# Sums of weight blocks kept as a rounded and a low half, in a three-stage hybrid layer on one core

## The chip, the cores and the metric

The kernel runs on one core of one Trainium2 chip. The metric is the device time of one execution in microseconds (us), as the median of several runs. PE is TensorE's matmul, PEld its weight load, DVE is VectorE, ACT ScalarE, POOL GpSimd, SP SyncE, which here only issues DMAs. "SPq" and "POOLq" are the DMA queues that SP and POOL feed.

## The reference, cut to what matters

One layer is applied to 2048 prompt tokens and to 64 tokens of a running sample. Nearly all the arithmetic is in matrix products with weights of 1024 rows:

```python
h = rms_norm(x, g_pre)
vA, bA, cA, zA, q, f, iv, zB, gA, gB = split_cols(h @ w_in)      # ten blocks of 1024 columns
yA = (silu(zA) * bA * causal_conv3(cA * vA)) @ w_a_out
S, o = hgrn2_scan(S0, silu(q) * scale, 1 - fg, iv, log(fg))      # chunks of 64 tokens, fg from f
yB = (norm(o) * g_onorm * silu(zB)) @ w_b_out
out = (sigmoid(gA) * yA + sigmoid(gB) * yB) @ w_o
x = x + rms_norm(out, g_post)
y = x + (p @ w_ple_proj) * sigmoid(rms_norm(x, g_ple) @ w_ple_gate)
```

All values are fp32.

## The kernel before, in words

**Products in three parts.** TensorE is fed in fp32r, a rounded fp32. So each fp32 operand is split into a rounded half `hi` and the remainder `lo` (`split`, lines 183 and 184: ACT rounds, DVE subtracts), and each product is made of three matmuls, hi with x_hi, hi with x_lo and lo with x_hi (lines 357 to 359, 490 to 492, 523 to 525). The weights are the stationary side, 128 x 128 at a time; a block of weights is a tile of 128 x 512, 256 KB: four 128 x 128 pieces. One such block with 352 tokens is twelve matmuls.

**Seven products for eight.** The 2112 tokens are cut into three blocks of 704, and each block into two halves of 352. Two weight columns (i1, i2), two halves of the depth and two halves of the tokens make a 2 x 2 by 2 x 2 product, which is done with seven block products in place of eight. Their weight sides are in `PRODUCTS` (lines 67 to 75), in the order A11, S3, S1, S2, A12, A22, S4. A11, A12 and A22 are blocks of the weights themselves. S1 to S4 are sums:

```
S1 = A21 + A22    S2 = S1 - A11    S3 = A11 - A21    S4 = A12 - S2
```

`sgroup` (line 343) does one such group. In blocks 1 and 2, `in_turn` (line 464) does W_A and W_B (in block 2 also W_O) product by product: all four groups' A11, then all their A12, then S2, S3, A22, S1 and S4 (`IN_TURN`, line 79), so four blocks of one kind stand in a row. The rest of W_O and the gate weights W_G go through plain `gemm`s.

**Keeping the sums.** Sums are made once. In block 0 `combined(first=True)` (line 286) loads four raw blocks, makes the four sums on DVE, and `keep_sum` (line 268) stores each sum to DRAM as plain fp32, splits it, and stores its low half (`split_w`, line 220). For W_A, W_B (in block 0) and W_O (in block 1) `prepare_sums` (line 303) does this beside other work, on POOL's queue; its `keep` (line 317) stores the sum, makes the low half in place and stores it. Later blocks load them: `kept_w` (line 274) loads the plain sum into a `raw` tile (line 194), ACT rounds it into a `hi` tile (line 214), and the low half is loaded into a `lo` or `s` tile (line 215). Blocks of the weights proper take the same way, from `w_blk`.

**Buffers.** All weight tiles are 128 x 512 of one pool `wp`: 5 for `raw`, 4 for `hi`, 4 for `lo`, 3 for `s` (`sum_tile`). Low halves in later blocks alternate between `lo` and `s` (`low_tile`, line 199), which gives seven buffers for seven products. A buffer is given out again once every reader of its last content is done. A scheduler lays out the order of each engine's instructions from dependences and priorities; every queue runs strictly in the order that results, so a DMA issue on SP that waits for a buffer holds up those behind it.

**Order of the work.** Block 0: `p @ w_ple_proj` for two blocks, heads with gates beside them (path B, to about 470 us of the span), path A (to about 690), the products with W_A, W_B and W_O by plain `gemm`s with `prepare_sums` beside them. Its last `gemm_by_k` (line 554) holds two weight columns, four `hi` tiles, to its end. Then gates of the next block (the first of them, `by_k`, line 361, goes through A11, S3, S1, S2 piece by piece), the end of the block with W_G, heads, path A, W_A and W_B in turn, W_O by plain `gemm`s; block 2 ends with W_A, W_B, W_O in turn, the last norm and W_G.

Of the kernel before, what the change touches and what calls it, by code (L numbers as in the profile page):

```python
# [10 lines left out]
F32 = mybir.dt.float32  # L11
F32R = mybir.dt.float32r
I32 = mybir.dt.int32
AF = mybir.ActivationFunctionType
ALU = mybir.AluOpType
# [3 lines left out]
P = 128  # L19
# [63 lines left out]
def hybrid_step(  # L83
# [17 lines left out]
    V, A, G, T, SP = nc.vector, nc.scalar, nc.gpsimd, nc.tensor, nc.sync  # L101
# [4 lines left out]
    wp = ctx.enter_context(tc.tile_pool(name="wp", bufs=4))  # L106
    ring = ctx.enter_context(tc.tile_pool(name="ring", bufs=RING))
    small = ctx.enter_context(tc.tile_pool(name="small", bufs=4))
    dram = ctx.enter_context(tc.tile_pool(name="dram", bufs=1, space=DRAM))
# [5 lines left out]
    def nm(s):  # L115
        uid[0] += 1
        return f"{s}_{uid[0]}"

    def rt(n=BN, dt=F32):
        t = ring.tile([P, BN + 4], dt, tag="r", name=nm("r"))  # L120
        return t if n is None else t[:, :n]
# [61 lines left out]
    def split(src, hi, lo):  # L183
        return A.copy(hi, src).ins, V.tensor_tensor(lo, src, hi.bitcast(F32), ALU.subtract).ins  # L184
# [7 lines left out]
    def load_raw(src):  # L192
        raw = wp.tile([P, 4, P], F32, tag="raw", name=nm("raw"), bufs=5)
        SP.dma_start(raw, src)
        return raw

    lows, turn = {}, [0]

    def low_tile():

        turn[0] += 1
        if turn[0] % 7 in (1, 3, 5):
            return sum_tile(F32R)
        return wp.tile([P, 4, P], F32R, tag="lo", name=nm("lo"))

    def sum_tile(dt=F32):
        return wp.tile([P, 4, P], dt, tag="s", name=nm("s"), bufs=3)

    def split_w(raw, key=None):

        hi = wp.tile([P, 4, P], F32R, tag="hi", name=nm("hi"))
        if key in lows:
            lo = low_tile()
            A.copy(hi, raw)  # L214
            SP.dma_start(lo.bitcast(F32), lows[key])
            return hi, lo
        lo = wp.tile([P, 4, P], F32R, tag="lo", name=nm("lo"))
        split(raw, hi, lo)
        if key is not None:
            lows[key] = dram.tile([P, 4, P], F32, tag=f"lo{key}", name=nm("low"), bufs=1)  # L220
            SP.dma_start(lows[key], lo.bitcast(F32))
        return hi, lo
# [42 lines left out]

    sums = {}

    def keep_sum(name, i1, s):

        sums.setdefault(i1, {})[name] = dram.tile([P, 4, P], F32, tag=f"{name}_{i1}", name=nm(name), bufs=1)  # L270
        SP.dma_start(sums[i1][name], s)
        return split_w(s, (i1, name))

    def kept_w(i1, i2, name, anew=False):

        keys = dict(A11=(i1, 0), A12=(i1, 1), A22=(i2, 1))
        if name in keys:
            return split_w(load_raw(w_blk[keys[name]]), None if anew else keys[name])
        return split_w(load_raw(sums[i1][name]), (i1, name))

    def combined(i1, i2, first):

        with tc.high_priority():
            if not first:
                return {n: kept_w(i1, i2, n) for _, n, _, _, _ in PRODUCTS}
            a11, a21, a22, a12 = (load_raw(w_blk[i, h]) for i, h in ((i1, 0), (i2, 0), (i2, 1), (i1, 1)))
            out = dict(A11=split_w(a11, (i1, 0)))

            def total(name, x, y, op):
                s = sum_tile()  # L290
                V.tensor_tensor(s, x, y, op)
                out[name] = keep_sum(name, i1, s)
                return s

            total("S3", a11, a21, ALU.subtract)
            s1 = total("S1", a21, a22, ALU.add)
            s2 = total("S2", s1, a11, ALU.subtract)
            out["A12"] = split_w(a12, (i1, 1))
            out["A22"] = split_w(a22, (i2, 1))
            total("S4", a12, s2, ALU.subtract)  # L300
            return out

    def prepare_sums(firsts, ahead):


        groups = [(idx + g, idx + KH + g) for idx in firsts for g in range(KH)]

        def tile_of(dt=F32):
            return rt(4 * P, dt).rearrange("p (k c) -> p k c", c=P)

        def load(i1, i2):
            out = [tile_of() for _ in range(4)]
            for t, (i, h) in zip(out, ((i1, 0), (i2, 0), (i2, 1), (i1, 1))):
                G.dma_start(t, w_blk[i, h])
            return out

        def keep(name, i1, s):
            sums.setdefault(i1, {})[name] = dram.tile([P, 4, P], F32, tag=f"{name}_{i1}", name=nm(name), bufs=1)
            lows[i1, name] = dram.tile([P, 4, P], F32, tag=f"lo{name}_{i1}", name=nm("low"), bufs=1)
            G.dma_start(sums[i1][name], s)  # L320
            lo = sum_tile(F32R) if ahead else tile_of(F32R)
            split(s, lo, lo)
            G.dma_start(lows[i1, name], lo.bitcast(F32))

        nxt = load(*groups[0])
        yield
        for n, (i1, _) in enumerate(groups):
            a11, a21, a22, a12 = nxt
            if ahead and n + 1 < len(groups):
                nxt = load(*groups[n + 1])  # L330
            V.tensor_tensor(a22, a21, a22, ALU.add)
            keep("S1", i1, a22)
            V.tensor_tensor(a21, a11, a21, ALU.subtract)
            keep("S3", i1, a21)
            V.tensor_tensor(a11, a22, a11, ALU.subtract)
            keep("S2", i1, a11)
            V.tensor_tensor(a12, a12, a11, ALU.subtract)
            keep("S4", i1, a12)
            if not ahead and n + 1 < len(groups):
                nxt = load(*groups[n + 1])  # L340
            yield
# [122 lines left out]
    def in_turn(stages, operand):  # L464
# [10 lines left out]
        for i, (st, n) in enumerate(todo):  # L475
# [3 lines left out]
            for g in range(KH):  # L479
                i1, i2 = st["idx"] + g, st["idx"] + KH + g  # L480
                with tc.high_priority():
                    hi, lo = kept_w(i1, i2, IN_TURN[n][0], IN_TURN[n][0] in st["anew"])
# [837 lines left out]
    for bi, bl in enumerate(blocks):  # L1320
# [6 lines left out]
        cols, a_first = [], []  # L1327
        rows = row_rstd(nxt, cols) if nxt else iter(())
        sums_ahead = prepare_sums((W_A, W_B), True) if first else prepare_sums((W_O,), False) if bi == 1 else iter(())

        def side(rows, sums_):
# [17 lines left out]
        else:  # L1349
            parts = [None] * KB  # L1350
# [89 lines left out]
```

## Time and profile before

| | before |
|---|---|
| runs, us | 2657.28, 2664.5, 2667.55; median 2664.5 |
| profiled execution, span, us | 2661.4 (no device time of its own is given beside the span) |
| mean granted TensorE clock | 0.997 |
| sums loaded from DRAM in later blocks | 392 of 256 KB |
| sums stored in block 0 by `keep_sum`, by `prepare_sums` | 160, 48 |
| DMA bytes | 735.00 MB, mean 276 GB/s |

The profile's page lists the busy time of each engine, groups of instructions by line (`out<-in xcount | busy us, mean ns | idle before`), and DMA issues (`KB each, median us to landing`). Other views are tables of busy time by stage, lists of who waited for whom (us in total, times, longest), and the instructions of one tile with the least, median and longest time from a DMA's issue to its landing.

### The profile page before, as it was taken

Reading aid. Unit: us, or ns where it says so; the run is one execution under the profiler, and the core shown is the slowest. Engines: PE = TensorE matmul, PEld = TensorE weight load, DVE = VectorE, ACT = ScalarE, POOL = GpSimd, SP = SyncE. Lnnn points to the kernel's source line nnn. Section 1 sums busy time; section 2 is a strip of 40 time slices with the busy share of each in tenths; the row PEclk is TensorE's granted clock in tenths of the full one; section 3 lists DMA queues with packets and bytes.
Section 4 is the critical chain, followed back from the end, with each engine's and each line's share of the span. In section 5 each row is a group of like instructions: output and inputs, shape, how many; then the busy total and the mean of one; then the engine's idle time right before and its main releaser. Section 6 shows DMA issues by size and latency. Waiting matters only on the chain.

```text
span 2661.4 us, 47775 instructions
## 1 busy us (share of the span) xinstructions
PE 2623.0 (99%) x16748; PEld 2600.4 (98%) x16748; DVE 1727.0 (65%) x3341; ACT 1449.6 (54%) x2782; POOL 349.1 (13%) x649
## 2 busy tenths in 40 slices
PE   7999999999999999999999999999999999999998
PEld 7999999999999999999999999999999999999988
DVE  7788888998667545466645578443355564447857
ACT  5655655454334544566645565454566654445664
POOL 1000000100432210001112210021000000001011
PEclk9999999999999999999999999999999999999999
DMA  8677777898998988776789988599867678889975
GB/s 304 217 263 269 244 260 271 299 316 288 367 344 285 352 289 275 252 227 221 222 287 357 391 304 306 182 352 307 276 218 222 222 224 263 273 274 319 302 234 168
DMA packets 362097, 735.00 MB, mean 276 GB/s; under 512 B 44064, under 2 KB 48704, under 8 KB 361856
## 3 DMA queue, kind: packets, MB, share of 16 engines
q1 hardware_dynamic: 324864, 588.20, 65.9%
q0 software_dynamic: 36704, 143.70, 14.9%
q8 instruction: 132, 2.16, 0.3%
q14 instruction: 109, 0.89, 0.1%
q10 hardware_dynamic: 288, 0.05, 0.0%
HBM read 525.71 MB, written 206.06 MB: 275 GB/s over the span
## 4 chain that ended last, share of the span: by engine, by line
PE 88%; DMA 4%; issue 3%; DVE 3%; ACT 1%; POOL 1%; SPq 0%; DVEq 0%; ACTq 0%; POOLq 0%
PE pg L357 19%; PE pg L358 19%; PE pg L359 19%; PE pg L523 4%; PE pg L525 4%; PE pg L524 4%; PE pg L491 3%; PE pg L490 3%; PE pg L492 3%; PE pa L957 1%; PE pa L921 1%; PE pa L911 1%; PE pa L959 1%; PE pa L910 1%; DMA low<-s 1%
## 5 line engine op out<-in xcount | busy, mean ns | idle before, releaser
L357 PE MATMUL pg<-r,hi 128*128 128x352 f32 x3304 | 1095.0, 332 | 6.8 <-DVE r L403 2.7
L358 PE MATMUL pg<-r,hi 128*128 128x352 f32 x3304 | 1070.1, 324 | 0.0
L359 PE MATMUL pg<-r,lo 128*128 128x352 f32 x2356 | 763.6, 324 | 0.0
L214 ACT CAST hi<-raw 128x512 fp32r<-128x512 f32 x708 | 435.6, 619 | 573.1 <-PE pg L358 206.5
L357 PEld LDWEIGHTS pg<-r,hi 128*128 128x128 f32 x3304 | 624.3, 189 | 12.6 <-DVE r L865 4.6
L358 PEld LDWEIGHTS pg<-r,hi 128*128 128x128 f32 x3304 | 623.9, 189 | 0.0
L359 PEld LDWEIGHTS pg<-r,lo 128*128 128x128 f32 x2356 | 443.9, 188 | 0.0
L359 PE MATMUL pg<-r,s 128*128 128x352 f32 x948 | 306.9, 324 | 0.0
L523 PE MATMUL pg<-r,hi 128*128 128x352 f32 x896 | 289.4, 325 | 3.1 <-ACT r L1194 2.1
L524 PE MATMUL pg<-r,hi 128*128 128x352 f32 x896 | 289.8, 324 | 0.6 <-DVE r L184 0.6
L525 PE MATMUL pg<-r,lo 128*128 128x352 f32 x756 | 244.6, 324 | 0.4 <-DVE lo L184 0.2
L184 ACT CAST hi<-raw 128x512 fp32r<-128x512 f32 x234 | 143.4, 619 | 165.4 <-PE pg L358 48.3
L184 DVE TENSOR_TENSOR r<-r,r 128x352 fp32r<-128x352 f32 (+3 forms) x274 | 169.9, 638 | 60.7 <-ACT r L184 60.0
L184 DVE TENSOR_TENSOR lo<-raw,hi 128x512 fp32r<-128x512 f32 x234 | 159.6, 688 | 65.8 <-ACT hi L184 54.2
L184 ACT CAST r<-r 128x352 fp32r<-128x352 f32 (+3 forms) x274 | 150.4, 578 | 75.1 <-DVE r L666 18.2
L184 ACT CAST hi<-s 128x512 fp32r<-128x512 f32 x160 | 99.1, 619 | 154.8 <-PE pg L358 132.7
L491 PE MATMUL pg<-r,hi 128*128 128x352 f32 x560 | 181.8, 326 | 0.0
L359 PEld LDWEIGHTS pg<-r,s 128*128 128x128 f32 x948 | 178.9, 189 | 0.1
L490 PE MATMUL pg<-r,hi 128*128 128x352 f32 x560 | 178.4, 326 | 0.1
L523 PEld LDWEIGHTS pg<-r,hi 128*128 128x128 f32 x896 | 168.0, 188 | 5.5 <-ACT r L1194 2.4
L524 PEld LDWEIGHTS pg<-r,hi 128*128 128x128 f32 x896 | 168.6, 188 | 2.0 <-DVE r L184 1.7
L371 ACT COPY hf<-pg 128x352 f32<-128x352 f32 x354 | 156.0, 446 | 6.9 <-PE pg L359 6.3
(358 smaller groups left out, 4096.9 us busy)
## 6 DMA issues: line engine op xcount, KB each, us to landing
raw<-w_blk SPq DMA_DIRECT2D x590, 256.0 KB, 4.0
lo<-low SPq DMA_DIRECT2D x404, 256.0 KB, 3.9
raw<-S SPq DMA_DIRECT2D x392, 256.0 KB, 4.1
low<-lo SPq DMA_DIRECT2D x346, 256.0 KB, 3.8
s<-low SPq DMA_DIRECT2D x304, 256.0 KB, 3.9
S<-s SPq DMA_DIRECT2D x160, 256.0 KB, 3.3
r<-w_blk POOLq DMA_DIRECT2D x48, 256.0 KB, 7.3
S<-r POOLq DMA_DIRECT2D x48, 256.0 KB, 6.1
```

Source lines behind the costliest of these rows:

```text
L184: return A.copy(hi, src).ins, V.tensor_tensor(lo, src, hi.bitcast(F32), ALU.subtract).ins
L214: A.copy(hi, raw)
L357: add(hi[:, k, :], xhi, start=start and k == 0, stop=False)
L358: add(hi[:, k, :], xlo, start=False, stop=False)
L359: last[0] = add(lo[:, k, :], xhi, start=False, stop=k == KH - 1).ins
L371: copied = A.copy(got[n], ps[bank])
L490: add(hi[:, k, :], xhi, start=start and k == 0, stop=False)
L491: add(hi[:, k, :], xlo, start=False, stop=False)
L492: last[0] = add(lo[:, k, :], xhi, start=False, stop=k == KH - 1).ins
L523: T.matmul(ps, hi[:, k % 4, :], xhi[:, c], start=k == ks[0], stop=False)
L524: T.matmul(ps, hi[:, k % 4, :], xlo[:, c], start=False, stop=False)
L525: last[0] = T.matmul(ps, lo[:, k % 4, :], xhi[:, c], start=False, stop=k == ks[-1]).ins
```

## The change

A sum is no longer stored as plain fp32. It is split first, and its rounded half is stored beside its low half. Later blocks load the rounded half straight into the tile that the matmuls read: for S2 and S3 a `hi` tile, for S1 and S4 a `raw` tile, with no cast by ACT. In `prepare_sums` the rounded half is made in an `s` tile, or in a ring tile where `ahead` is false, and the low half in place of the sum, and the DVE sums of a group move ahead of the first store.

```diff
+    def keep_hi(name, i1, hi, queue):
+        sums.setdefault(i1, {})[name] = dram.tile([P, 4, P], F32, tag=f"{name}_{i1}", name=nm(name), bufs=1)
+        queue.dma_start(sums[i1][name], hi.bitcast(F32))
+
     def keep_sum(name, i1, s):
-        sums.setdefault(i1, {})[name] = dram.tile([P, 4, P], F32, tag=f"{name}_{i1}", name=nm(name), bufs=1)
-        SP.dma_start(sums[i1][name], s)
-        return split_w(s, (i1, name))
+        parts = split_w(s, (i1, name))
+        keep_hi(name, i1, parts[0], SP)
+        return parts
+
+    def kept_sum(name, i1):
+        if name in ("S2", "S3"):
+            hi = wp.tile([P, 4, P], F32R, tag="hi", name=nm("hi"))
+        else:
+            hi = wp.tile([P, 4, P], F32R, tag="raw", name=nm("raw"), bufs=5)
+        lo = low_tile()
+        SP.dma_start(hi.bitcast(F32), sums[i1][name])
+        SP.dma_start(lo.bitcast(F32), lows[i1, name])
+        return hi, lo

     def kept_w(i1, i2, name, anew=False):
...
-        return split_w(load_raw(sums[i1][name]), (i1, name))
+        return kept_sum(name, i1)
...
         def keep(name, i1, s):
-            sums.setdefault(i1, {})[name] = dram.tile([P, 4, P], F32, tag=f"{name}_{i1}", name=nm(name), bufs=1)
             lows[i1, name] = dram.tile([P, 4, P], F32, tag=f"lo{name}_{i1}", name=nm("low"), bufs=1)
-            G.dma_start(sums[i1][name], s)
-            lo = sum_tile(F32R) if ahead else tile_of(F32R)
-            split(s, lo, lo)
-            G.dma_start(lows[i1, name], lo.bitcast(F32))
+            hi = sum_tile(F32R) if ahead else tile_of(F32R)
+            split(s, hi, s.bitcast(F32R))
+            keep_hi(name, i1, hi, G)
+            G.dma_start(lows[i1, name], s)
...
             V.tensor_tensor(a22, a21, a22, ALU.add)
+            V.tensor_tensor(a21, a11, a21, ALU.subtract)
+            V.tensor_tensor(a11, a22, a11, ALU.subtract)
             keep("S1", i1, a22)
-            V.tensor_tensor(a21, a11, a21, ALU.subtract)
             keep("S3", i1, a21)
-            V.tensor_tensor(a11, a22, a11, ALU.subtract)
+            V.tensor_tensor(a12, a12, a11, ALU.subtract)
             keep("S2", i1, a11)
-            V.tensor_tensor(a12, a12, a11, ALU.subtract)
             keep("S4", i1, a12)
```

## The prediction, before any run of the changed kernel

> **What bounds the kernel now.** I read the page's head and busy parts first, then the busy table by stage, then the list of what TensorE waited for.
>
> ```profile
> span 2661.4 us, 47775 instructions
> PE 2623.0 (99%) x16748; PEld 2600.4 (98%) x16748; DVE 1727.0 (65%) x3341; ACT 1449.6 (54%) x2782; POOL 349.1 (13%) x649
> PEclk9999999999999999999999999999999999999999
> ```
> ```profile
> 0.00:60.00 60.00, 47.72 (x258) 44.94 (x258) 46.75 (x94) 35.84 (x79) 9.88 (x21) 0.97 0.86 306
> 60.00:470.00 410.00, 401.78 (x2645) 395.59 (x2646) 342.56 (x675) 234.99 (x436) 30.51 (x50) 1.00 0.73 254
> 470.00:700.00 230.00, 230.00 (x1435) 229.94 (x1434) 202.08 (x355) 115.53 (x222) 33.16 (x63) 1.00 0.89 306
> 2560.00:2661.00 101.00, 89.72 (x550) 86.23 (x549) 69.32 (x144) 50.64 (x110) 14.08 (x23) 0.99 0.55 179
> ```
> ```profile
> PE pa L614 <- DVE r L633: 3.1, 2, 1.7
> PE pg L357 <- ACT hi L214: 1.5, 2, 0.7
> PE pg L523 <- ACT hi L184: 0.5, 1, 0.5
> PE pg L524 <- DVE r L184: 0.2, 1, 0.2
> ```
>
> The second fence gives for a stage: its length, then busy time (and instructions) of PE, weight load, DVE, ACT and POOL, then clock, DMA share, GB/s. The third lists PE's waits between 830 and 1800 us: total, times, longest. The reader is to see that PE is the bound, at full clock. Busy PE alone would not prove it is moving, but 470 to 700 is nearly all 352-column products: 230.00 / 1435 = 0.160 us each, so one product of twelve matmuls (one weight block) takes 1.92 us. PE is idle for 2661.4 - 2623.0 = 38.4 us in all, of which 12.3 lie in the first 60 us, 8.2 from 60 to 470 and 11.3 in the last 101. Kept sums are loaded only between these, so at most 38.4 - 31.8 = **6.6 us** can be won. What can be lost has no such bound: PE wants a high and a low block of 256 KB every 1.92 us, and each late block stops it.
>
> **The casts that go.**
>
> ```profile
> L214 ACT CAST hi<-raw 128x512 fp32r<-128x512 f32 x708 | 435.6, 619 | 573.1 <-PE pg L358 206.5
> raw<-S SPq DMA_DIRECT2D x392, 256.0 KB, 4.1
> S<-s SPq DMA_DIRECT2D x160, 256.0 KB, 3.3
> low<-lo SPq DMA_DIRECT2D x346, 256.0 KB, 3.8
> S<-r POOLq DMA_DIRECT2D x48, 256.0 KB, 6.1
> ```
>
> 392 sums are loaded (98 groups of four), and each now takes no cast: ACT loses 392 x 0.619 = 243 us of its 1449.6. The order of the built program agrees: 392 ACT instructions fewer, none fewer on PE, DVE, POOL or SP. ACT is not the bound, so the 243 us are worth only the PE waits that they cause. Of the waits above, 1.5 us are on such a cast. The 3.1 us on L633 are a norm whose squares stand on ACT behind casts that wait for loads; blocks straight from w_blk keep their casts there, so I take half. **Gain 3.0 us**; nothing at the least, 4.6 at the most. No DMA byte is saved: a rounded and a low half are as long as a sum and a low half.
>
> **The stores.** In block 0 the 160 stores of sums wait for ACT's rounding instead of DVE's sum, and hold one of four high buffers until they land; behind them on SP stand raw loads and low stores. The 346 low stores already hold one of four low buffers in just this way and follow a cast by one DVE operation, and PE did not wait on them. Cast 0.6 + landing 3.3 is 3.9 of the four products, 7.7 us, that a high buffer is busy anyway. Cost nothing; if a store landed over 3.8 us later than that, the excess would go to PE, once for each such store. The 48 stores that POOL issues wait for a cast too, and come after two or three sums instead of one. Their readers are a stage away; behind them on POOL's queue stand the loads of the next group but one, or of the next. I take 0, and -2 to +2 as bounds.
>
> **The loads, where the price lies.** Before, a sum landed in one of five raw buffers and waited there. When PE left a high buffer, only a cast of 0.62 us stood between release and the next use; the 206.5 us that casts waited for PE in the L214 row show the data lying ready. Now S2 and S3 land in the four high buffers themselves, so a whole transfer must fit between the release of the buffer and its use. S1 and S4 take raw buffers, which mostly come free far earlier (over 100 matmuls, 16 us). A stall is
>
> issue + landing - (matmuls between release and use) x 0.160.
>
> The matmuls are counted in the order of the built program. Of the 196 S2 and S3 loads 48 have 49 (7.8 us; S3 within a group waits for the last S2, with A12, A22, S4 and A11 between), the rest of those in groups mostly more; 24 have 37 (5.9 us; all S2 and S3 of the in-turn stages stand in a row, so three products lie between); a few have far fewer. Two have 17 (2.7 us): the first S2 of blocks 1 and 2, where the last W_O gemm holds all four buffers to its end. One has 13 (2.1 us): the first S3 of W_B in block 1, whose buffer comes from an S2 that ends late. In the same W_B one S2 has 27 (4.3 us) and one S4 29 (4.6 us); an S3 in block 2's W_B has 24 (3.8 us). Behind a load that waits, SP holds the next low and high blocks, which are used after it and have more room.
>
> For landing I take raw tiles in the windows 860:900, 1700:1750, 1615:1640, 1640:1660, 2460:2510, 1545:1580 and 1420:1480, in this order, and for the issue the last fence:
>
> ```profile
> DMA to landing us min/median/max: 3.1/5.3/11.2
> DMA to landing us min/median/max: 2.8/4.6/11.5
> DMA to landing us min/median/max: 3.1/4.2/5.5
> DMA to landing us min/median/max: 4.2/5.9/6.7
> DMA to landing us min/median/max: 2.6/4.1/8.3
> DMA to landing us min/median/max: 2.5/4.7/9.5
> DMA to landing us min/median/max: 4.6/7.4/9.6
> ```
> ```profile
> L194 SPq DMA_DIRECT2D raw<-S x80: 319/320/1331, 1370.0 to 1638.0; - x80
> ```
>
> With medians and 0.3 us for the issue:
> - first S2 of block 1: 5.3 + 0.3 - 2.7 = 2.9; of block 2: 4.6 + 0.3 - 2.7 = 2.2.
> - W_B of block 1: first S3 4.2 + 0.3 - 2.1 = 2.4; the S2 0.2; the S4 5.9 + 0.3 - 4.6 = 1.6.
> - W_B of block 2: 4.1 + 0.3 - 3.8 = 0.6.
> - the loads with 5.9 us: 4.7 + 0.3 fits in the median. The longest, 9.5, does not; I choose 1.0 in all, since a stalled PE gives the loads after it the same time.
> - path A of block 1 from 1420 to 1480: some four S3, 7.4 + 0.3 against 7.8. Half of them are over, by at most 9.6 + 0.3 - 7.8 = 2.1; at 1.0 each, 2.0.
>
> **Losses 12.9 us.** Bounds: with the smallest landing of each window the single places give 0.7 + 0.4 + 1.3 + 0 and nothing else, 2.4. With the largest they alone give 8.8 + 9.1 + 3.7 + 1.5 + 2.4 + 4.8 = 30.3. I stay at the medians, since these windows hold the very loads in question.
>
> The Trainium skill, "DMA: Bandwidth & Descriptors", section "Anatomy of one DMA — SWDGE (gpsimd) path", fits a transfer as about 2.0 us plus its bytes at 436 GB/s, which by estimate is 2.6 us for one of these blocks; the trace shows that only as a minimum (2.5), and by that figure alone the losses would shrink to about 1.2 us.
>
> **The sum.** 12.9 - 3.0 = +9.9 us on the profiled execution: span 2671.3. The page gives no device time beside that span; it stands 3.1 us under the median of the runs, 2664.5, and inside their range (2657.28 to 2667.55). On the median: **2674.4 us**, 0.4% slower. About 0.5%, 13.3 us, is what a measurement here can tell from no change.
>
> **Rivals.**
>
> *The loads are hidden, only ACT's relief remains.* For it: five raw buffers for S1 and S4 and only three casts in seven let SP run further ahead, so the queue may be shorter when a late S2 or S3 is issued, with landing near the minima above. Against it: PE's appetite is the same, and the DMA share in this stretch is 95 to 98%:
>
> ```profile
> 1367.00:1480.00 113.00, 0.00 (x0) 0.00 (x0) 1.00 0.98 349
> 1480.00:1640.00 160.00, 61.44 (x194) 36.09 (x194) 1.00 0.95 336
> ```
>
> It gives 2.4 - 4.6 = -2.2 to 2.4 - 0 = +2.4, so 2662 to 2667, not slower.
>
> *The high buffers bind over whole stages (slower).* In the in-turn stages four buffers circulate; each takes issue + landing + 1.92 us a round, and a round may last 4 x 1.92 = 7.7 us. From a landing of 5.5 us PE is paced by it. In block 1's W_A and W_B the rows above have 4.2 to 5.9, and POOL's transfers share the same engines. At path A's 7.4 a product would take (0.3 + 7.4 + 1.92) / 4 = 2.4 us, 0.48 more, times 16 S2 and S3: 7.7 us. Path A itself decides from 7.5 us: at 8.5 (between median and longest) each of block 1's 16 S3 loses 1.0 us, 14 more than I counted. Together 2674.4 + 7.7 + 14 = **2696 us**. For it: the rows' longest landings; against: block 0's and block 2's stages have room, and every stall lets the queue drain.
>
> That the change does not do what it says is excluded by the order: the casts are gone, and the matmuls read the landed tiles.
>
> **Chances.** The forecast (2668 to 2680) 0.45; the loads hidden 0.25, with a small part beyond -0.5%, since even all 6.6 us of idle time are only 0.25%; the buffers binding 0.30. Faster by over 0.5%: 0.03, for something that I do not see. Slower by over 0.5%, above 2677.8: the binding case and the upper edge of the forecast, 0.35. Within: 0.62. The range takes in the hidden case with the scatter of the runs and most of the binding one: 2659 to 2694.
>
> **What would show it.** ACT near 1449.6 - 243 = 1207 us with 2390 instructions; the L214 group 316 instead of 708. PE busy within a few us of 2623, its idle time near 48 instead of 38. In PE's waits new rows on loads of S2 and S3 into hi, together some 10 us, in a handful of places: near 865, 1625, 1650 and 1720. The L214 wait of 1.5 gone, L633 halved. Bytes 735 MB as before. Wrong: if such rows are missing (first rival), if they come by the dozen at 0.5 to 2 us between 1370 and 1640 (second), or if PE idles before 470, which the stores would have to explain.

## The result, and the profile after

| | before | after |
|---|---|---|
| median of the runs, us | 2664.6 | 2703.09 |
| runs, us | 2657.28 to 2667.55 | 2698.77 to 2708.24 |
| span of the profiled execution, us | 2661.4 | 2704.2 |

The ratio is 1.0145, with a 95% interval of 1.0122 to 1.0167: the change makes the kernel 1.45% slower, 38 us. The forecast was 2674.4 us with a range up to 2694. The sign is as forecast and the size is not: the profiled span grew by 42.8 us where the sum gave 9.9. (The medians differ by 38.5 us; each profile is of one execution.)

First the head and the busy part of the page of after, then the groups and DMA issues that answer to the rows of before.

```profile
span 2704.2 us, 46995 instructions
PE 2636.9 (98%) x16748; PEld 2608.7 (96%) x16748; DVE 1729.9 (64%) x3341; ACT 1231.0 (46%) x2390; POOL 350.2 (13%) x649
...
L214 ACT CAST hi<-raw 128x512 fp32r<-128x512 f32 x316 | 195.7, 621 | 389.2 <-PE pg L372 202.2
...
raw<-S SPq DMA_DIRECT2D x196, 256.0 KB, 3.8
hi<-S SPq DMA_DIRECT2D x196, 256.0 KB, 3.8
S<-hi SPq DMA_DIRECT2D x160, 256.0 KB, 3.4
```

The change does what it says: 392 casts are gone, and 392 loads land where the matmuls read. ACT is relieved of 218.6 us. But PE is idle for 2704.2 - 2636.9 = 67.3 us instead of 38.4, and it is busy for 13.9 us longer with the same 16748 matmuls. 28.9 + 13.9 = 42.8.

Where the idle time lies is read from the busy table by stage, first of before, then of after (length, PE, weight load, DVE, ACT, POOL, clock, DMA share, GB/s).

```profile
833.00:940.00 107.00, 104.14 (x643) 102.24 (x642) 64.41 (x99) 63.00 (x117) 17.42 (x30) 0.98 0.86 309
1360.00:1640.00 280.00, 279.90 (x1732) 278.45 (x1731) 173.14 (x352) 158.52 (x330) 52.54 (x113) 1.00 0.96 342
1640.00:1800.00 160.00, 157.30 (x967) 155.29 (x968) 88.78 (x150) 86.42 (x164) 20.68 (x37) 0.98 0.77 269
2450.00:2560.00 110.00, 110.00 (x680) 108.45 (x679) 83.94 (x182) 70.20 (x149) 10.51 (x19) 1.00 0.91 300
```
```profile
833.00:940.00 107.00, 101.89 (x619) 99.76 (x618) 60.11 (x92) 47.23 (x89) 17.47 (x30) 0.97 0.82 293
1360.00:1640.00 280.00, 269.68 (x1634) 266.61 (x1633) 164.54 (x329) 106.79 (x235) 52.17 (x113) 0.98 0.92 322
1640.00:1800.00 160.00, 152.98 (x942) 149.07 (x941) 90.54 (x159) 70.03 (x137) 17.34 (x31) 1.00 0.74 257
2450.00:2560.00 110.00, 99.22 (x581) 97.10 (x579) 78.55 (x167) 42.49 (x94) 9.56 (x18) 0.95 0.81 276
```

In path A of block 1 and the in-turn stage behind it (1360 to 1640) PE did 98 matmuls fewer in the same 280 us, in block 2's last in-turn stage (2450 to 2560) 99 fewer in 110 us. DMA share and GB/s fell as well, so the transfers did not slow PE by taking more of the engines: PE's stalls left them less to do.

Since every version runs the same 16748 matmuls in nearly the same order, the start of the n-th matmul of after can be set beside that of before in the two traces. The shift, with the growth that each stage adds (times of before):

| stage | shift at its end, us | added |
|---|---|---|
| start to 840, block 0 | -3.4 | -3.4 |
| 840 to 1098, border and gates of block 1 | 2.6 | +6.0 |
| 1098 to 1393, path B of block 1 | 2.5 | 0 |
| 1393 to 1586, path A of block 1, `prepare_sums` for W_O beside it | 13.0 | +10.5 |
| 1586 to 1652, W_A and W_B in turn | 22.0 | +9.0 |
| 1652 to 1800, W_O, start of block 2 | 23.5 | +1.5 |
| 1800 to 2398, block 2's paths | 24.8 | +1.3 |
| 2398 to the end, in turn | 42.6 | +17.8 |

And what PE waited for between 833 and 2560 in after (total, times, longest):

```profile
PE pg L504 <- DMA hi<-S: 8.5, 5, 4.8
PE pg L371 <- DMA hi<-S: 7.9, 6, 2.2
PE pg L505 <- DVE r L184: 7.2, 3, 3.8
PE pa L628 <- DVE r L647: 3.5, 2, 1.8
PE pg L371 <- ACT hf L385: 2.3, 4, 1.1
PE pg L371 <- DVE r L417: 2.0, 1, 2.0
PE pg L504 <- DMA raw<-S: 1.4, 1, 1.4
```

Two things are to be seen. 16.4 us in eleven waits are for S2 and S3 to land in a high buffer; that kind was forecast. Another 11.5 us are waits for DVE and ACT (the rows with L184, L385 and L417), none of which stands in this stretch of before at more than 0.5 us. They are no direct wait on a sum at all.

The longest of the waits on L184 (3.8 of the 7.2 us) is followed back in the timeline of after between 2466 and 2490: ACT, then what SP issues, then PE (start, length, engine and line, the wait before it in brackets).

```profile
2476.48 0.62 ACT L184 CAST hi<-raw 128x512 fp32r<-128x512 f32 x1 [2.06 <-DMA raw<-w_blk]
2483.88 0.62 ACT L184 CAST hi<-raw 128x512 fp32r<-128x512 f32 x1 [5.61 <-DMA raw<-w_blk]
2484.40 0.48 ACT L184 CAST r<-r 128x352 fp32r<-128x352 f32 x1
...
2473.80 0.33 SPq L194 DMA_DIRECT2D raw<-w_blk  x1
2475.74 2.99 SPq L194 DMA_DIRECT2D raw<-w_blk  x3
...
2486.58 0.66 PE L505 MATMUL pg<-r,hi 128*128 128x352 f32 x1 [3.80 <-DVE r L184]
```

These are blocks straight from w_blk, which open the next weight's group and still take the old way through a raw buffer and a cast. SP asks for them only at 2473.8 to 2478.7, as raw buffers come free, because S1s and S4s now sit in raw buffers until PE has read them. ACT works in order, so it stands 5.61 us before a cast whose block has not landed. Behind that cast in ACT's order stands the rounding of an operand (2484.40), DVE's remainder waits for the rounding, and PE waits for the remainder.

### The profile page after: what moved, and what is told of

Its sections match the earlier page's. It is cut to its first block, busy times and chain, and to the rows that moved or that the text cites. A ratio compares the mean times of both kernels' runs of the same rounds, so it can differ in the third digit from the quotient of the medians.

```text
span 2704.2 us, 46995 instructions
## 1 busy us (share of the span) xinstructions
PE 2636.9 (98%) x16748; PEld 2608.7 (96%) x16748; DVE 1729.9 (64%) x3341; ACT 1231.0 (46%) x2390; POOL 350.2 (13%) x649
## 5 line engine op out<-in xcount | busy, mean ns | idle before, releaser
L371 PE MATMUL pg<-r,hi 128*128 128x352 f32 x2680 | 889.4, 332 | 17.6 <-DMA hi<-S 7.9
L372 PE MATMUL pg<-r,hi 128*128 128x352 f32 x2680 | 867.4, 324 | 0.0
L371 PEld LDWEIGHTS pg<-r,hi 128*128 128x128 f32 x2680 | 505.5, 189 | 26.0 <-issue 7.7
L372 PEld LDWEIGHTS pg<-r,hi 128*128 128x128 f32 x2680 | 505.7, 189 | 0.0
L214 ACT CAST hi<-raw 128x512 fp32r<-128x512 f32 x316 | 195.7, 621 | 389.2 <-PE pg L372 202.2
L537 PE MATMUL pg<-r,hi 128*128 128x352 f32 x896 | 289.0, 324 | 3.4 <-ACT r L1208 2.1
L538 PE MATMUL pg<-r,hi 128*128 128x352 f32 x896 | 289.8, 324 | 0.4
L184 ACT CAST hi<-raw 128x512 fp32r<-128x512 f32 x234 | 143.6, 621 | 182.4 <-PE pg L538 51.3
L184 DVE TENSOR_TENSOR r<-r,r 128x352 fp32r<-128x352 f32 (+3 forms) x274 | 169.8, 638 | 76.3 <-ACT r L184 76.0
L184 DVE TENSOR_TENSOR lo<-raw,hi 128x512 fp32r<-128x512 f32 x234 | 159.9, 689 | 81.6 <-ACT hi L184 72.7
L371 PE MATMUL pg<-r,raw 128*128 128x352 f32 x624 | 207.6, 333 | 0.0
L372 PE MATMUL pg<-r,raw 128*128 128x352 f32 x624 | 201.8, 323 | 0.0
L385 ACT COPY hf<-pg 128x352 f32<-128x352 f32 x354 | 155.7, 448 | 84.0 <-PE pg L373 83.5
L184 ACT CAST r<-r 128x352 fp32r<-128x352 f32 (+3 forms) x274 | 148.5, 580 | 91.4 <-DVE r L680 18.1
L537 PEld LDWEIGHTS pg<-r,hi 128*128 128x128 f32 x896 | 167.9, 188 | 5.4 <-ACT r L184 2.4
L184 ACT CAST hi<-s 128x512 fp32r<-128x512 f32 x160 | 99.3, 621 | 158.5 <-PE pg L372 120.2
L538 PEld LDWEIGHTS pg<-r,hi 128*128 128x128 f32 x896 | 168.4, 188 | 1.8 <-DVE r L184 1.7
```

Source lines behind the costliest of these rows:

```text
L371: add(hi[:, k, :], xhi, start=start and k == 0, stop=False)
L372: add(hi[:, k, :], xlo, start=False, stop=False)
L385: copied = A.copy(got[n], ps[bank])
L537: T.matmul(ps, hi[:, k % 4, :], xhi[:, c], start=k == ks[0], stop=False)
L538: T.matmul(ps, hi[:, k % 4, :], xlo[:, c], start=False, stop=False)
```

## The experiments

Theory at the start: a buffer that PE reads directly is given out later, and the landing no longer fits before its use (**high buffers** for S2 and S3, theory H in the expectations; **raw buffers** for S1 and S4, and through these the w_blk blocks, theory R). Rivals: the stores in block 0; POOL's transfers in the in-turn stages; ACT's casts standing in order before late loads. Each ratio is to before on the same chip, so ratios are compared and not times; shifts are worked out as in the table above.

**1. Only the stores.** Sums are stored as after does, and loaded through `raw` and a cast as before does.

```diff
-        return kept_sum(name, i1)
+        return split_w(load_raw(sums[i1][name]), (i1, name))
```


> Stores as in the changed kernel (rounded halves), loads as before (into a raw tile, then ACT's cast into a high tile). Theory 'the loads cost it, the stores nothing': 2660 to 2670 us, as before. Rival 'the stores delay block 0 or the kept halves': more than half of the 38 us stays, 2683 or more.

Measured: 2670.03 us, ratio 1.0018 (1.0007 to 1.0028), 4.8 us by the ratio. The shift rises by 7.3 us in path A of block 1 and does not grow in the in-turn stages. So the stores that were costed at nothing cost about 5 us when alone. The waits between 1395 and 1560, first of before, then of this run:

```profile
DVE r L331 <- DMA r<-w_blk: 23.7, 4, 6.9
```
```profile
DVE r L345 <- DMA r<-w_blk: 29.0, 4, 8.5
PE pg L371 <- DVE r L417: 4.9, 3, 2.7
```

DVE waits longer for a raw block that POOL asked for behind the stores, now later by a cast and by two or three sums; DVE too works in order, and the sinks of path A (L417, additions on finished products), on which PE waits, stand behind it.

**2. That cause by itself.** The first run again, but in `prepare_sums` the next group's blocks are asked for ahead of the stores for W_O too.

```diff
-            if ahead and n + 1 < len(groups):
+            if n + 1 < len(groups):
                 nxt = load(*groups[n + 1])
...
-            if not ahead and n + 1 < len(groups):
-                nxt = load(*groups[n + 1])
```


> Stores alone changed (2670.0), but the next group of raw blocks for W_O's sums in block 1 is asked for ahead of the group's stores on POOL's queue. If the 6 us of that run come from DVE waiting, in its order, for blocks that POOL asks for behind the later stores (8.5 us longest wait against 6.9 before): 2663 to 2667. If they come from elsewhere: 2670.

Measured: 2662.73 us, ratio 0.9999 (0.9989 to 1.0009). The 5 us are gone: DVE waits 8.3 us for these blocks in place of 29.0, and the shift no longer rises in path A of block 1 (0.3 us). The loads now go out earlier than in before, too, where DVE waited 23.7 us without holding up PE. So the stores' share comes from the place of each next group's four loads in POOL's queue.

**3. Only the loads.** The stores of before, and plain sums loaded directly into what the matmuls read.

```diff
-        return split_w(load_raw(sums[i1][name]), (i1, name))
+        return kept_sum(name, i1)
```


> The other half of the change alone: plain sums are stored as before, and loaded as they are multiplied (what is multiplied as the high half is the unrounded sum here; all else is computed as in the changed kernel). The run with the stores alone cost 5.9 us, 6 of them in path A of block 1. If the parts add up: 2703 - 6 = 2697, and the shift in path A of block 1 falls from 10 to about 4. If the loads bring out what the stores did anyway: 2703 again.

Measured: 2701.7 us, ratio 1.0138 (1.0108 to 1.0169). Nearly the whole loss is in the loads: path A of block 1 adds 3.8 us, the in-turn stages 9.8 and some 17. Whether the stores' 5 us come on top can't be told from the times: 1.0138 and 0.0018 make 1.0156, and both this and 1.0138 lie in the interval of after (1.0122 to 1.0167).

**4. S1 and S4 alone, S2 and S3 alone.** The other pair goes through `raw` and a cast. The edit is that of the first kernel; the second has ("S1", "S4") in its place.

```diff
     def kept_w(i1, i2, name, anew=False):
...
+        if name in ("S2", "S3"):
+            return split_w(load_raw(sums[i1][name]), (i1, name))
         return kept_sum(name, i1)
```


> Only S1 and S4 are loaded as they are multiplied, into raw tiles; S2 and S3 go through the cast. Theory H (four high buffers, release to use shorter than a landing): 2662 to 2670, nearly nothing is lost. Theory R (S1 and S4 hold raw buffers until PE has read them, so that the blocks from w_blk behind them are asked for late and ACT waits for them in its order): 2680 to 2695, with the waits for narrowed operands at the start of W_B and W_O still there.

> Only S2 and S3 are loaded as they are multiplied, into high tiles; S1 and S4 go through the cast. Theory H: 2690 to 2705, nearly all is lost here. Theory R: 2672 to 2685, the waits on loads into high tiles remain, those on narrowed operands at the start of W_B and W_O go. If both hold, the losses of this and of the run with S1 and S4 alone add up to about 38.

Measured: S1 and S4 alone 2702.47 us, 1.0138 (1.012 to 1.0155); S2 and S3 alone 2715.2 us, 1.0188 (1.017 to 1.0206). The halves do not add up: one half alone costs as much as the whole change, the other more, and each more than its own theory gave it. So neither theory holds alone. PE's waits between 833 and 2580 of the run with S1 and S4, then of the run with S2 and S3:

```profile
PE pg L507 <- DVE r L184: 9.9, 8, 2.8
PE pa L630 <- DVE r L649: 8.7, 2, 4.7
PE pg L373 <- DVE r L419: 7.9, 3, 4.0
```
```profile
PE pg L373 <- DMA hi<-S: 28.3, 11, 6.5
PE pg L506 <- DMA hi<-S: 8.0, 5, 3.5
```

Each half shows one mechanism without the other, but harder than it is in after, since the pair that goes through the cast takes buffers that it does not take there. With S1 and S4 in raw buffers, through which S2 and S3 now pass as well, no sum is loaded into a high buffer, and PE waits on DVE behind ACT: ACT's casts wait 63.7 + 41.5 + 18.1 = 123.3 us for raw blocks in this run, 46.1 in before and 58.2 in after. With S2 and S3 direct and all other five blocks cast into the same four high buffers, only 37 matmuls, 37 x 0.160 = 5.9 us, lie by the order of the program between release and use of an S2 or S3 in all groups (49 to 61 in after, whose S1 and S4 use no high buffer), and the waits on landings rise from 16.4 to 36.3 us.

**5. The in-turn stages through the cast,** the groups direct.

```diff
-    def kept_w(i1, i2, name, anew=False):
+    def kept_w(i1, i2, name, anew=False, cast=False):
...
+        if cast:
+            return split_w(load_raw(sums[i1][name]), (i1, name))
         return kept_sum(name, i1)
...
-                    hi, lo = kept_w(i1, i2, IN_TURN[n][0], IN_TURN[n][0] in st["anew"])
+                    hi, lo = kept_w(i1, i2, IN_TURN[n][0], IN_TURN[n][0] in st["anew"], True)
```


> The groups of seven load all four sums as they are multiplied, the in-turn stages go through the cast as before. By the shift of PE's work between the two traces the in-turn stages cost about 27 of the 43 us (9 in block 1, 18 in block 2): if that is a cost of these stages themselves, 2672 to 2680. If it is inherited from what path A leaves behind, 2690 or more.

Measured: 2678.8 us, 1.0052 (1.0031 to 1.0072). The in-turn stages add -0.1 and 0.7 us, so about 24 us of the loss belong to these two short stages. Path A of block 1 keeps 9.3.

**6. More buffers.** Each needs room from the ring of `r` tiles, so the first of the four is a control: RING 50 for 52 and nothing else. Then six high buffers with ring 50, seven raw buffers with ring 50, and both with ring 49. The same numbers of buffers are set wherever such a tile is taken.

```diff
-RING = 52
+RING = 49
...
-            hi = wp.tile([P, 4, P], F32R, tag="hi", name=nm("hi"))
+            hi = wp.tile([P, 4, P], F32R, tag="hi", name=nm("hi"), bufs=6)
...
-            hi = wp.tile([P, 4, P], F32R, tag="raw", name=nm("raw"), bufs=5)
+            hi = wp.tile([P, 4, P], F32R, tag="raw", name=nm("raw"), bufs=7)
...
```


> The changed kernel with 50 ring tiles in place of 52, which the next two kernels need for room: a control. 2700 to 2706 if the ring isn't tight; anything above is to be taken off the next two.

> The changed kernel with six high buffers (ring 50). Counted in the order of the program, a load of S3 in path A's groups gets 85 matmuls (13.6 us) between release and use in place of 49 (7.8 us), one of S2 or S3 in the in-turn stages about 60 (9.6 us) in place of 37 (5.9 us); raw tiles stay as they are. Theory H (distance of the high buffers): the waits on loads of S2 and S3 into hi go, at the borders too, and 12 to 18 us of the 38 with them: 2685 to 2691. Theory R (raw buffers): 2700.

> The changed kernel with seven raw buffers (ring 50). The blocks from w_blk that open W_B and W_O get 73 matmuls (11.7 us) in place of 49 (7.8 us), S4 in the in-turn stages 73 to 120 in place of 49; the high buffers stay as they are. Theory R: the waits for narrowed operands at the start of W_B and W_O (2.9 and 3.8 us, and the slow clock behind them) go, 10 to 15 us: 2688 to 2693. Theory H: 2700.

> The changed kernel with six high and seven raw buffers (ring 49). Six high buffers alone were slower (2741): the waits on loads into hi went, but ACT waited 228 us for raw blocks from w_blk instead of 58, since the casts came up to 35 matmuls behind the release of their raw buffer, and held up ACT's copies. Theory 'two distances' (release of the high buffer to use, and release of the raw buffer to cast, in the order of the program): with seven raw buffers the second is 83 matmuls in the groups, so there both are long and only the in-turn stages lose (13 matmuls there between release and cast of the blocks that open W_B and W_O): 2675 to 2690. Rival 'loads in this order congest whatever the buffers': 2700 or more.

| | us | ratio to before | waits on hi<-S, us | growth of the shift from 840 to the end, us |
|---|---|---|---|---|
| after | 2703.09 | 1.0145 (1.0122 to 1.0167) | 16.4 | 46.0 |
| ring 50 | 2707.99 | 1.0168 (1.0148 to 1.0189) | 23.5 | 49.7 |
| seven raw | 2703.27 | 1.0152 (1.0129 to 1.0175) | 22.8 | 38.3 |
| six high | 2741.43 | 1.0294 (1.0272 to 1.0317) | none among the leading | 61.2 |
| both | 2688.94 | 1.0092 (1.0069 to 1.0116) | none among the leading | 8.3 |

The control lies 2 us above the range expected for it, but its interval overlaps that of after. The expectation for six high buffers failed outright: the waits on landings went, and the kernel became some 38 us slower than after, 34 by the ratios than the control. The waits between 833 and 2560 of that run show why, and then two rows of what ACT waited for in the whole span:

```profile
PE pa L628 <- DVE r L647: 16.0, 2, 8.2
PE pg L505 <- DVE r L184: 13.4, 10, 3.4
PE pg L371 <- DVE r L417: 10.5, 3, 4.5
```
```profile
ACT hi L214 <- DMA raw<-w_blk: 156.3, 59, 11.4
ACT hi L184 <- DMA raw<-w_blk: 71.4, 29, 6.6
```

By the order of the program ACT may with six high buffers cast a w_blk block 85 matmuls ahead of its use, but with five raw buffers that block is asked for at most 120 ahead: 35 matmuls, 5.6 us, are left for the landing. In the trace between 1395 and 1560 PE does 21 to 60 matmuls between the issue of such a load and its cast, 49 to 82 in the run with both. ACT then stands before a cast that nobody needs yet (227.7 us in all), and what is needed stands behind it. Seven raw buffers alone do the reverse, though the time missed what theory R gave (2688 to 2693). ACT's waits for raw blocks fall to 20 us and PE's on L184 to 2.8, from 69.8 and 7.2 in the control, but those on landings in high buffers stay as in the control:

```profile
PE pg L371 <- DMA hi<-S: 14.8, 7, 4.1
PE pg L504 <- DMA hi<-S: 8.0, 5, 3.9
PE pg L505 <- DVE r L184: 2.8, 4, 0.8
```

From 840 on that is 38.3 us where the control has 49.7. The whole time can't be told from the control's, since this version comes out of block 0 some 10 us later than the control (5.0 against -4.8 at 840), most of it in the first 85 us, which I didn't follow up.

Only both together remove both, and in full only in the groups of seven. The waits between 833 and 2560 of that run:

```profile
PE pg L504 <- ACT r L184: 3.1, 2, 1.6
PE pg L506 <- DMA lo<-low: 1.7, 1, 1.7
PE pg L371 <- DVE r L417: 1.5, 2, 0.8
```

From 840 on its shift grows by 8.3 us, where that of after grows by 46.0. Of block 0's delay 5.6 us are won back by 940; path A of block 1 adds 2.2 us instead of 10.5, the stages from 2398 on still 10.5 instead of 17.8, as was expected of the in-turn stages: PE waits 1.60 us at 2472 and 3.69 at 2582 (in W_O, behind the window above) for operands that ACT rounds late. And block 0 has already cost 18.4 us by 775. The smaller ring does not show as the reason, since the control stands at -3.2 us there. Seven raw buffers alone have 6.6 us there, all of it from the first 85 us, six high buffers 9.2, of which 8 come between 85 and 470; the run with both has both (7.1 at 85, 15.8 at 470). Why larger pools cost block 0 that, and whether ring 49 adds to it, no run separates. The landings were no faster with both. The DMA issues between 1360 and 1640, first of after, then with six and seven buffers:

```profile
hi<-S SPq DMA_DIRECT2D x38, 256.0 KB, 4.4
```
```profile
hi<-S SPq DMA_DIRECT2D x42, 256.0 KB, 5.3
```

5.3 us without a wait, 4.4 us with waits: it is the distance between release and use that decides, not the speed of the transfer.

**7. Only the groups direct, with six high, seven raw, ring 49.** `prepare_sums`, the order of its sums too, and the in-turn stages are as before: the edits of run 5 and of the last kernel of run 6, and

```diff
         def keep(name, i1, s):
...
-            hi = sum_tile(F32R) if ahead else tile_of(F32R)
-            split(s, hi, s.bitcast(F32R))
-            keep_hi(name, i1, hi, G)
-            G.dma_start(lows[i1, name], s)
+            sums.setdefault(i1, {})[name] = dram.tile([P, 4, P], F32, tag=f"{name}_{i1}", name=nm(name), bufs=1)
...
+            G.dma_start(sums[i1][name], s)
+            lo = sum_tile(F32R) if ahead else tile_of(F32R)
+            split(s, lo, lo)
+            G.dma_start(lows[i1, name], lo.bitcast(F32))
...
```

> The part of the change that looked harmless, with room: only the groups' sums (made in block 0) are kept as rounded halves and loaded as they are multiplied; W_A, W_B and W_O keep plain sums and casts; six high and seven raw buffers, ring 49. Theory 'two distances': no loss is left, 2660 to 2667, at best some us under the kernel before. Rival 'congestion': 2675 or more.

Measured: 2669.97 us, 1.0026 (1.0015 to 1.0038). Between 833 and 2560 PE waits on nothing for more than 0.2 us in total, and the shift falls from 17.9 at 840 to 8.2 at the end. Where there is room, direct loads cost PE no wait; but the time lies 3 us above the range expected, since block 0 comes out about as late as in the run with both. So no version tried beats before; run 2, which keeps the casts, equals it.

**8. Without POOL's reloads of the gates beside W_A and W_B.**

```diff
+            if n == 1:
+                tiles.extend(rt() for _ in range(KH))
+                for t in tiles[-KH:]:
+                    G.memset(t, 1.0)
-            if kind is not None:
+            elif kind is not None:
```


> The changed kernel without POOL's reload of half the gates after the second product of W_A and W_B; a memset stands in its place, so these gates are 1 and the output is another. These four transfers of 352 KB run beside the first loads of S2 in the in-turn stages. If the waits there (1.9, 0.9 and 4.8 us on loads into hi) are made by that burst, they shrink to below 1 us and the time falls by 5 to 10 us, to 2693 to 2698. If they come from the short release alone (37 matmuls, 5.9 us): within 3 us of 2703.

Measured: 2697.97 us, 1.0134 (1.0111 to 1.0158). It was tried because of the longest wait of after, 4.79 us at 2517. What DMAs were issued there, between 2496 and 2526 of after, with the median to landing (two of the four gate tiles are shown), and from the timeline of after the matmul that waited:

```profile
hi<-S SPq DMA_DIRECT2D x8, 256.0 KB, 6.7
...
r<-g__5124_22174 POOLq DMA_DIRECT2D x1, 352.0 KB, 6.4
...
r<-g__5304_23198 POOLq DMA_DIRECT2D x1, 352.0 KB, 8.3
```
```profile
2517.02 0.63 PE L504 MATMUL pg<-r,hi 128*128 128x352 f32 x1 [4.79 <-DMA hi<-S]
```

That matmul is the first on S3 in W_B. Without the reloads it does not wait; the eight landings there have a median of 4.9 us, and the only such wait left between 2450 and 2560 is 3.1, on the S2 before it. Two transfers of 352 KB (`r<-p_fm`), which POOL issues right behind the gates in after, stay in this run. But the interval overlaps that of after, and the waits on high buffers in the groups (L371) are 13.6 us in place of 7.9. The reloads lengthen single stalls; that they are the cause of the 38 us is not borne out.

## Why the prediction was wrong, point by point

- **The bound** was read rightly: at most 6.6 us to win, no such limit to what can be lost.
- **Gain 3.0 us**: half right. The 1.5 us on L214 are gone. The norm's 3.1 us (L633, now L647) did not halve but are 3.5. Its squares no longer stand behind casts that wait for loads, but behind one that waits for PE to leave a buffer, here and at 1803.80 (3.35 us):

```profile
923.91 0.62 ACT L214 CAST hi<-raw 128x512 fp32r<-128x512 f32 x1 [3.19 <-PE pg L372]
```

  The copy on ACT (L385) that PE waits 1.13 us for at 906.26 stands behind such a cast too, which waits 6.94 us for PE. So the casts that are left still hold up what stands behind them on ACT. ACT's busy time falls by 218.6 us instead of 243, with 392 casts fewer as counted: the casts' durations fall by 242.1 us in sum, but the busy time counts instructions that overlap once. It lies off the path.
- **Stores at nothing, -2 to +2**: wrong, 4.8 us alone. "Their readers are a stage away" held. What failed was the look at what stands behind the 48 stores on POOL's queue: it was named and then taken at 0, though the blocks for W_O are asked for only after them and DVE waits for these in order.
- **S2 and S3, single places**: right in kind and place, and nearly in size but for one. The waits of after in the order of time:

```profile
864.10 0.40 PE L371 MATMUL pg<-r,hi 128*128 128x352 f32 x1 [1.84 <-DMA hi<-S]
...
1644.28 0.40 PE L504 MATMUL pg<-r,hi 128*128 128x352 f32 x1 [1.85 <-DMA hi<-S]
...
1673.32 0.40 PE L504 MATMUL pg<-r,raw 128*128 128x352 f32 x1 [1.39 <-DMA raw<-S]
...
1746.11 0.40 PE L371 MATMUL pg<-r,hi 128*128 128x352 f32 x1 [1.33 <-DMA hi<-S]
```

  1.84 for 2.9, 1.85 for 2.4, 1.39 for the S4's 1.6, 1.33 for 2.2. The one is the S3 of W_B in block 2, 4.79 for 0.6, the wait of run 8: its load goes out at 2508.38, when PE has read the second S2, with 24 matmuls left as counted, and takes 8.5 us to land where 4.1 was put in. The bounds had it at 4.8, with the longest landing of its window. When one block is late PE pays that block's landing, not the median.
- **The loads with 5.9 us of room, 1.0 in all**: 0.58 and 0.40 us in block 1's W_A and 0.91 in block 2's, 1.9 in all; near enough.
- **Path A of block 1, 2.0 us**: 2.09 + 2.19 us at 1486 and 1516 are such waits on S3, twice what was forecast; the rest of the stage's 10.5 us is in the stores' wait of 1.96 us at 1457, in the clock and in smaller waits.
- **Losses 12.9 us**: all waits on landings of rounded halves in after, the two rows on hi<-S and the S4's 1.4, make 17.8. This term was 4.9 short, most of it by that one S3; it explains little of the 33 us that the sum missed.
- **The step that failed** is this: "S1 and S4 take raw buffers, which mostly come free far earlier", with "behind a load that waits, SP holds the next low and high blocks, which are used after it and have more room". I counted the room of S1 to S4 and of nothing else. The blocks from w_blk share the raw buffers and SP's queue; in the in-turn stages the distance from release to use of the next A11's raw buffer fell, by the order of the program, from 96 matmuls to 49. They are late for ACT, and ACT hands the delay on through its order: 7.2 us of PE's waits (L184), and with two of them 13.7 us at half clock, for which the sum had nothing. The first kernel of run 4 shows S1 and S4 alone at 37 us (with the new stores, and with S2 and S3 in the raw buffers too), and seven raw buffers take most of the waits on L184 away (2.8 us instead of 7.2), while those on landings in high buffers stay.
- **PE busy within a few us of 2623**: wrong, 2636.9. No term stood for it. Between 830 and 2560 the clock record of after has 27.3 us at half clock, that of before 10.2. The matmuls then start 0.293 us apart instead of 0.160; 75 do so in after and 28 in before, and 47 more at that pace are 6.3 us, while 17.1 us more of slow clock could cost at most 17.1 x (1 - 0.160 / 0.293) = 7.8. The rest of the 13.9 is not settled in detail; part of it is that the first matmul after a stall counts 0.40 to 0.66 us, as the rows above show.
- **The rivals.** "The loads are hidden" fell. "The high buffers bind over whole stages" came nearest with 2696, by a mechanism that is only half of what happened: between 1360 and 1660 there are only five waits on hi<-S, 7.1 us in all, and six high buffers alone made the time worse.

Open: how the 10.5 us of path A split between late stores and late loads. Alone they add 7.3 and 3.8 us, 11.1 together, but PE's waits there differ: on the sinks 2.0 us in after and 4.9 with the stores alone, on landings in high buffers 4.4 in after and 0.6 with the loads alone. Open too are the share of the clock beyond the bounds above and what the larger pools cost in block 0.

## What to carry to other kernels

A cast between a landing buffer and the buffer that TensorE reads is also a buffer stage: before removing it, count for every user of both pools, not only for the tiles that change, the matmuls between release and next use, and set them beside the long landings rather than the median. An engine that runs in order hands a late load on to work that has nothing to do with it, so list what stands behind each wait. More buffers in one pool let that engine commit earlier to loads that the other pool can't supply; the pools must grow together, and here the versions with both larger still came out slower than before.

## What the runs showed of the hardware

In after the granted TensorE clock fell to one half during or within about 2 us of six stalls of TensorE between 830 and 2560, of 1.65 to 4.79 us, for 3.4 or 6.8 us. The windows of after that lie inside such stretches (length, PE and its matmuls, weight load, DVE, ACT, POOL, clock, DMA share, GB/s):

```profile
865.00:868.00 3.00, 3.00 (x12) 3.00 (x12) 0.00 (x0) 0.00 (x0) 0.00 (x0) 0.50 0.02 9
1517.00:1520.00 3.00, 3.00 (x12) 3.00 (x12) 2.15 (x6) 1.43 (x3) 0.32 (x2) 0.50 0.93 338
2487.00:2493.00 6.00, 5.91 (x20) 5.46 (x20) 5.34 (x12) 1.93 (x5) 0.00 (x0) 0.50 0.76 278
```

These go with the waits that end at 864.10 (1.84 us), 1516.09 (2.19) and 2486.58 (3.80). The wait of 2.09 us that ends at 1486.62 is followed by no such stretch. So a stall can cost more than its length. The clock record puts the starts of these stretches at 864.94, 1516.89 and 2486.27, 191 x 3.413 and 284 x 3.413 us apart. The Trainium skill, "TensorE: Matmul & The Clock Gate", Part 1 on the clock gate, gives half rate as the state after an idle window of about 3.4 us, with windows that run freely. The lengths of the stretches agree, and so do their starts, which stand whole windows of 3.413 us apart; the idle time here was shorter than that, 1.65 us being enough in one place (at 927.66) and 2.09 not in another.
